# Sixteen gate columns by seven block products instead of eight, with their operands, results and the branch outputs passed through DRAM

## The chip, the core and the metric

The kernel runs on one core of a Trainium2 chip. Five engines work side by side: TensorE (PE in the profile, with its weight loads PEld), VectorE (DVE), ScalarE (ACT), GpSimd (POOL) and SyncE (SP, which here only issues transfers between DRAM and the on-chip memory). The metric is the device time of one execution in microseconds (us); the kernel before has a median of 1602.3 us over three runs.

## The reference

One layer on 1024 tokens of width 1024, all in float32, with 16 meta tokens in front. Only the lines that the change concerns are given:

```python
a = rms_norm(h, norm_mix)
(q_na, k_na, v_na, q_hg, z_f, z_b, i_hg, g_hg, gate_na, gate_hg) = split_cols(a @ w_in)
y_na = neighbourhood_attention(q_na, k_na, v_na, rpb) @ w_na_out      # 512 -> 1024
y_hg = hgrn2_branch(q_hg, z_f, z_b, i_hg, g_hg, ...) @ w_hg_out       # 512 -> 1024
mix = sigmoid(gate_na) * y_na + sigmoid(gate_hg) * y_hg
h = h + mix @ w_o
h = h + square(relu(rms_norm(h) @ w_up)) @ w_down
```

The two gates are a 1024 x 1024 by 1024 x 2048 product: 16 blocks of 128 columns.

## The kernel before

Float32 products are made from three products of a rounded type: each operand is split into `hi` (a rounded copy, a cast on ACT) and `lo` (what is left, a subtraction on DVE), and PE adds hi*hi, hi*lo and lo*hi in one PSUM bank (`mm3`, lines 133 to 135). A weight block is 128 columns of `w_in` (1024 x 128): `load_block` (lines 117 to 125) issues its load on SP's queue into a `raw` tile and makes `hi` and `lo`. Two `raw`, two `hi` and two `lo` tiles of this kind exist (the pool `wp`).

The program has these stages. First the rows are normalised and transposed into `aT` (two tile pairs, for tokens 0 to 511 and 512 to 1023). Then come four HGRN heads (`hgrn`, four times some 85 us). A head doubles its block size over seven levels. At a level PE multiplies 128 x 128 blocks into `sc`, POOL updates `Y` (line 363), DVE makes the next `X` from it (lines 360 and 361) and the queries `QQ` (line 378). Before the levels POOL adds `kd` from `X` and `Y` twice, once for each half of the tokens (line 338), and DVE makes `q` from a projection (line 291). Projections of the next columns stand between these small matmuls as filler. Their results `oT` stay on chip. The neighbourhood attention (NA) follows, two heads at a time in four pairs, and its result `OT` stays on chip too.

The gates are ordinary projections (`gate_proj`, line 632): 16 blocks, each 2 halves of the tokens x 8 slices x 3 = 48 matmuls, 768 in all, and a sigmoid on ACT straight from PSUM into an on-chip tile `sg` (line 636). They are interleaved with the multiplication of the branch outputs by `w_hg` and `w_na`, the stage "mix" (384 matmuls), whose operands `sh` and `sl` are split from `oT` and `OT` on chip. After it come `w_o`, the second norm, `w_up` (which already uses seven block products, lines 797 to 935) and `w_dn`.

A scheduler fixes the order of the instructions on each engine, and on SP's queue, when the program is built. It works from its own estimates of what each costs; every engine then executes its list in that order, and an instruction that waits holds up all those behind it on its engine. (Only the last stage is in an order written by hand.)

Of the kernel before, what the change touches and what calls it, by code (L numbers as in the profile page):

```python
# [46 lines left out]
def layer(ctx: ExitStack, tc: tile.TileContext, x, meta, w_in, w_na, w_hg, w_o, w_up, w_dn,  # L47
# [173 lines left out]
    oTs = ExitStack()  # L221
    oTp = oTs.enter_context(tc.tile_pool(name="oTp", bufs=1, side="right"))
    oT = oTp.tile([P, NHG, T], F32, name="oT")
# [41 lines left out]
    def hgrn(hd, hp, lmask_get, gates, more):  # L265
# [172 lines left out]
        list(more)  # L438
        yield
        for hf in (1, 0):  # L440
# [39 lines left out]
    OTp = oTs.enter_context(tc.tile_pool(name="OTp", bufs=1, side="right", reuse_waits="tile"))  # L480
    psum_pools(mx=1, s=2, t=2, b=1)
    OT = OTp.tile([P, NPAIR, T], F32, name="OT")
    with tc.tile_pool(name="np", bufs=1, reuse_waits="tile") as npl:
# [17 lines left out]
        for p in range(NPAIR):  # L501
# [52 lines left out]
            po = {}  # L554

# [20 lines left out]
            def values(s, i, js, pr):  # L576
# [35 lines left out]
                dst = OT[64 * i:64 * i + 64, p].rearrange("p (r s c) -> p s r c", s=8, c=8)  # L612
# [9 lines left out]
            for st in pend:  # L622
                values(*st)


    psum_pools(mx=3, a=3)
    mixs = ExitStack()
    mixp = mixs.enter_context(tc.tile_pool(name="mixp", bufs=1, reuse_waits="tile"))
    sgp = mixs.enter_context(tc.tile_pool(name="sgp", bufs=4, reuse_waits="tile"))
    mix = mixp.tile([P, KC, T], F32, name="mix")  # L630

    def gate_proj(col):
        sg = sgp.tile([P, T], F32, tag="sg", name="sg")

        def ev(ps, t0, n):
            act.activation(sg[:, t0:t0 + n], ps, AF.Sigmoid)
        proj(col, ev)
        return sg

    gates = []  # L640
# [5 lines left out]
    for br, (wsrc, src) in enumerate(((w_hg, oT), (w_na, OT))):  # L646
        with tc.tile_pool(name="op", bufs=1, reuse_waits="tile") as op_:
            sh = op_.tile([P, 4, T], F32R, name="sh")
            sl = op_.tile([P, 4, T], F32R, name="sl")
            gates_to(8 * br + 2)  # L650
            for k in range(4):
                split(sh[:, k], sl[:, k], src[:, k])
# [68 lines left out]

# [93 lines left out]
    def up_bank(t):  # L815
        return bank(t, t).rearrange("p a b -> p (a b)")
# [389 lines left out]
```

## Time and profile before

| | |
|---|---|
| three runs | 1599.82, 1602.3, 1603.77 us |
| the profiled execution | 1602.57 us, with a span of 1600.4 us from the first to the last instruction (2.2 us lie around it) |
| input and norm | 0 to 38 us |
| HGRN heads, from the first level work on POOL | 38 to 397 us |
| NA | 397 to 615 us, gate matmuls as filler from 580 us |
| the rest of the gates and the mix | 615 to 862 us |
| `w_o`, second norm | 862 to 956 us |
| `w_up` | 956 to 1293 us |
| `w_dn`, last norm | 1293 to 1600 us |

A row of the page's groups or of the timeline names the line, the engine, the operation, output<-inputs with the shapes, and how often; then busy time, the mean time of one, and idle time of the engine before it with what ended it. In the windows view each row is a stretch of the span, with the busy time and the number of instructions of each engine, the granted clock of PE (1.00 is full) and the transfers.

### The profile page before, as it was taken

The page shows a single profiled execution, that of the slowest core. Times are in us where ns is not written, and L with a number is a line of the kernel's source. Part 1 is how long each engine was busy: PE and PEld are TensorE (multiplying, and loading weights), DVE is VectorE, ACT ScalarE, POOL GpSimd, SP SyncE. Part 2 cuts the span into 40 slices and gives each one's busy share as a digit, 9 for nine tenths or more (in the row PEclk, how much of TensorE's full clock was granted, in tenths as well). Part 3 has the DMA queues.
Part 4 walks back from the last instruction along what each step waited for, and adds up shares of the span by engine and source line. Part 5 has one row for each costly group of instructions (what it writes and reads, how often), then busy time and mean ns, then how long its engine had stood idle before and what let it go on. Part 6 is the DMA issues. An engine that isn't in the chain of part 4 may idle for free.

```text
span 1600.4 us, 20348 instructions
## 1 busy us (share of the span) xinstructions
PE 1555.2 (97%) x7876; PEld 1309.3 (82%) x7876; DVE 964.2 (60%) x1524; ACT 607.6 (38%) x1082; POOL 333.9 (21%) x299
## 2 busy tenths in 40 slices
PE   6999999999999999999999998999999999999998
PEld 5788889888888888888887876788888878887886
DVE  6666767565767865123226258766666454779666
ACT  6221121112656654112123035555555443434444
POOL 4322121212011000000000012543333300227033
PEclk9999999999999999999999999999999999999999
DMA  5101001002122111111412123544444477563324
GB/s 184 40 27 40 27 28 40 27 28 68 30 74 63 45 41 40 40 53 53 145 53 78 54 105 113 168 156 163 145 152 145 160 261 234 199 224 118 99 86 145
DMA packets 120625, 158.03 MB, mean 99 GB/s; under 512 B 6337, under 2 KB 80065, under 8 KB 120529
## 3 DMA queue, kind: packets, MB, share of 16 engines
q1 hardware_dynamic: 118624, 150.70, 28.7%
q10 hardware_dynamic: 1584, 4.98, 0.8%
q8 instruction: 62, 1.02, 0.3%
q0 software_dynamic: 320, 1.05, 0.2%
q14 instruction: 35, 0.28, 0.1%
HBM read 118.96 MB, written 37.75 MB: 98 GB/s over the span
## 4 chain that ended last, share of the span: by engine, by line
PE 86%; DVE 7%; issue 3%; ACT 2%; POOL 1%; DMA 1%; DVEq 0%; POOLq 0%; SPq 0%; ACTq 0%
PE mm L134 14%; PE mm L133 13%; PE mm L135 13%; PE mm L949 4%; PE pa L949 4%; PE pc L949 4%; PE sc L351 4%; PE pb L949 3%; PE pb L800 3%; PE pb L802 3%; PE pb L801 3%; PE pc L800 2%; PE pc L801 2%; PE pc L802 2%; PE pa L800 2%
## 5 line engine op out<-in xcount | busy, mean ns | idle before, releaser
L133 PE MATMUL mm<-aT,hi 128*128 128x512 f32 (+2 forms) x896 | 328.6, 367 | 1.2 <-DVE QX L507 1.2
L135 PE MATMUL mm<-aT,lo 128*128 128x512 f32 (+2 forms) x896 | 327.5, 366 | 0.1
L134 PE MATMUL mm<-aT,hi 128*128 128x512 f32 (+2 forms) x896 | 326.6, 364 | 0.0
L133 PEld LDWEIGHTS mm<-aT,hi 128*128 128x128 f32 x896 | 169.6, 189 | 23.5 <-issue 1.4
L135 PEld LDWEIGHTS mm<-aT,lo 128*128 128x128 f32 x896 | 169.4, 189 | 23.1 <-POOL lo L124 0.3
L134 PEld LDWEIGHTS mm<-aT,hi 128*128 128x128 f32 x896 | 169.5, 189 | 22.0
L95 DVE TENSOR_TENSOR dl<-ur,dh 128x1024 fp32r<-128x1024 f32 x55 | 76.5, 1392 | 93.7 <-ACT dh L94 91.8
L94 ACT CAST dh<-ur 128x1024 fp32r<-128x1024 f32 x55 | 57.9, 1053 | 162.3 <-issue 78.1
L123 ACT CAST hi<-raw 128x1024 fp32r<-128x1024 f32 x44 | 46.3, 1053 | 189.0 <-PE mm L134 171.2
L124 DVE TENSOR_TENSOR lo<-raw,hi 128x1024 fp32r<-128x1024 f32 x42 | 51.6, 1230 | 85.8 <-ACT hi L123 85.8
L90 POOL TENSOR_SCALAR rtm<-ssq 128x1 f32<-128x1 f32 (+1 forms) x17 | 7.5, 439 | 397.0 <-ACT junk L754 372.1
L812 DVE TENSOR_TENSOR wl<-sx,wh 128x512 fp32r<-128x512 f32 x70 | 50.0, 722 | 30.7 <-ACT wh L811 30.7
L811 ACT CAST wh<-sx 128x512 fp32r<-128x512 f32 x70 | 42.6, 620 | 64.9 <-PE pc L801 27.3
L812 DVE TENSOR_TENSOR wl<-raw,wh 128x512 fp32r<-128x512 f32 x46 | 50.2, 1091 | 23.8 <-ACT wh L811 23.0
L351 PE MATMUL sc<-QQ,X 128*128 128x128 f32 x448 | 61.7, 288 | 1.5 <-DVE QQ L378 1.2
L351 PEld LDWEIGHTS sc<-QQ,X 128*128 128x128 f32 x448 | 58.2, 196 | 4.4 <-issue 2.0
L363 POOL TENSOR_TENSOR Y<-X,TN 128x512 f32<-128x512 f32 x20 | 33.8, 1691 | 110.3 <-DVE X L360 110.3
L819 ACT ACTIVATE uv<-uv 128x512 f32<-128x512 f32 x48 | 30.4, 633 | 66.4 <-DVE uv L927 49.9
L932 POOL TENSOR_TENSOR us<-u,uv 128x512 f32<-128x512 f32 x15 | 24.3, 1619 | 137.5 <-ACT uv L820 137.5
L569 DVE CUSTOM_DVE_ANT_0 pr<-nsc,NB 128x432 f32<-128x432 f32 (+1 forms) x64 | 35.3, 559 | 28.1 <-PE nsc L564 27.9
L800 PE MATMUL pb<-nt,wh 128*128 128x512 f32 x128 | 50.3, 393 | 2.0 <-DVE uv L920 2.0
L551 POOL TENSOR_TENSOR NB<-NB,bs 128x256 f32<-128x256 f32 (+1 forms) x24 | 19.6, 842 | 156.3 <-DMA NB<-in_wmask 94.1
(331 smaller groups left out, 3906.3 us busy)
## 6 DMA issues: line engine op xcount, KB each, us to landing
ur<-usp SPq DMA_DIRECT2D x55, 512.0 KB, 3.3
raw<-in_w_in SPq DMA_DIRECT2D x48, 512.0 KB, 3.7
raw<-in_w_up SPq DMA_DIRECT2D x16, 1024.0 KB, 6.0
usp<-us SPq DMA_DIRECT2D x60, 256.0 KB, 2.1
w<-in_w_dn SPq DMA_DIRECT2D x16, 512.0 KB, 4.5
usp<-uv SPq DMA_DIRECT2D x30, 256.0 KB, 2.5
xt<-in_x SPq DMA_DIRECT2D x8, 512.0 KB, 9.3
hres<-in_x SPq DMA_DIRECT2D x8, 512.0 KB, 6.5
```

What stands on the lines that cost most here:

```text
L94: act.copy(hi, src)
L95: dve.tensor_tensor(lo, src, hi.bitcast(F32), op=ALU.subtract)
L124: eng.tensor_tensor(lo[:, :kc], raw[:, :kc], hi[:, :kc].bitcast(F32), op=ALU.subtract)
L133: pe.matmul(ps, lh, rh, start=first, stop=False)
L134: pe.matmul(ps, lh, rl, start=False, stop=False)
L135: pe.matmul(ps, ll, rh, start=False, stop=last)
L351: pe.matmul(sc[:, c], X[:, tb + c * P:tb + (c + 1) * P], fap(QQ, tb + c * P, [[2 * h, P // (2 * h)], [T + h, 2], [1, h]]), start=True, sto ...
L800: pe.matmul(ps, lhs[0][:, c], rhs[0][:, k], start=first and k == 0, stop=False, skip_group_check=True)
L801: pe.matmul(ps, lhs[0][:, c], rhs[1][:, k], start=False, stop=False, skip_group_check=True)
L802: pe.matmul(ps, lhs[1][:, c], rhs[0][:, k], start=False, stop=k == 3, skip_group_check=True)
L812: dve.tensor_tensor(v(lo), src, v(hi).bitcast(F32), op=ALU.subtract)
L949: pe.matmul(ps, a[n == 2][:, q, j * P:(j + 1) * P], b[n == 1][:, q], start=first and n == 0, stop=last and n == 2, skip_group_check=True)
```

## The change

Each pair of gate columns (2m, 2m+1) becomes one 2 x 2 block product: two halves of the inner dimension, two halves of the tokens, two column blocks. Strassen's scheme (Winograd's form) needs seven products of 12 matmuls (`chain`) where the plain form needs eight, so 8 x 84 = 672 matmuls in place of 768.

- Sums of the activations (`block_sums`): for each of four slices POOL restores four 128 x 512 blocks from `aT`'s hi and lo (four additions) and makes `t1`, `t2`, `t3`, `t4` of them (four subtractions). One slice is made in each HGRN head, and each result is stored in DRAM (`tsp`).
- Two of the seven products (`first_gates`) need no sums. They are written ahead of the others; the intermediate `g1` stays on chip, and the first sigmoid goes to DRAM.
- The other five (`gate_pair`) need the sums of the activations, read back and split (`second_operand`), and sums of the weights made on DVE (`gate_sums`, four 128 x 512 operations) that are then split. Additions on DVE and one on POOL put the products together before the sigmoid. All gates go to DRAM (`gsp`) and are read back in the mix.
- The branch outputs go to DRAM (`osp`) in place of `oT` and `OT`, and are read back and split ahead of the mix (`branch_operand`). The gates are now finished before the mix begins.

The stages `w_up` and `w_dn` are as before (helpers have only moved up in the file).

The diff, cut to its core:

```diff
-    oTs = ExitStack()
...
-    oT = oTp.tile([P, NHG, T], F32, name="oT")
...
+    def block_sums(k, pool_):
+        r = {}
+        for v, h, kk in (("t1", 0, k), ("t3", 1, k), ("t2", 1, k + 4), ("t4", 0, k + 4)):
+            r[v] = pool_.tile([P, TH], F32, tag="rt", name="rt", bufs=4)
+            hi, lo = (t[:, kk, :TH].bitcast(F32) for t in aT[h])
+            pool.tensor_tensor(r[v], hi, lo, op=ALU.add)
+        pool.tensor_tensor(r["t1"], r["t3"], r["t1"], op=ALU.subtract)
+        pool.tensor_tensor(r["t3"], r["t2"], r["t3"], op=ALU.subtract)
+        pool.tensor_tensor(r["t2"], r["t2"], r["t1"], op=ALU.subtract)
+        pool.tensor_tensor(r["t4"], r["t4"], r["t2"], op=ALU.subtract)
+        for v in r:
+            sp.dma_start(tsp[v][k], r[v])
...
+        block_sums(hd, hp)
...
-            dve.scalar_tensor_tensor(oT[:, hd, hf * TH:(hf + 1) * TH], pt.rearrange("p c t -> p (c t)"),
+            ot = hp.tile([P, TH], F32, tag="ot", name="ot", bufs=2)
+            dve.scalar_tensor_tensor(ot, pt.rearrange("p c t -> p (c t)"),
...
+            sp.dma_start(osp[0][hd][:, hf * TH:(hf + 1) * TH], ot)
...
-    OT = OTp.tile([P, NPAIR, T], F32, name="OT")
...
+            sp.dma_start(osp[1][p], OT)
...
+    g1 = {m: gfp.tile([P, TH], F32, name=f"g1_{m}") for m in reversed(range(NG))}
...
+    def gate_out(c, h, t, src):
+        act.activation(t, src, AF.Sigmoid)
+        sp.dma_start(gsp[c][:, h * TH:(h + 1) * TH], t)
+    def first_gates(ms):
+        blocks, ps = [], []
+        for m in ms:
+            hi, lo = load_block(w_in[:, gate_col(2 * m):gate_col(2 * m) + P], KC)
+            blocks.append([[flat(t)[:, q * TH:(q + 1) * TH] for t in (hi, lo)] for q in range(2)])
+        for m, b in zip(ms, blocks):
+            ps.append(mm_tile())
+            chain(ps[-1], b[0], aV["b11"], True)
+            act.copy(g1[m], ps[-1])
+        for m, b, p in zip(ms, blocks, ps):
+            chain(p, b[1], aV["b21"], False)
+            gate_out(2 * m, 0, gfp.tile([P, TH], F32, tag="go", name="go", bufs=2), p)
...
+    psum_pools(pa=2, pb=2, pc=2)
+    first_gates((0, 1))
+    first_gates((2, 3))
...
+    def second_operand(v):
+        for k in range(4):
+            t = g_tile("gv", TH, bufs=5)
+            sp.dma_start(t, tsp[v][k])
+            split(aV[v][0][:, k], aV[v][1][:, k], t)
...
+    def gate_sums(m):
...
+            c = gate_col(2 * m + q)
+            sp.dma_start(t, w_in[:, c:c + P].rearrange("(k p) c -> p k c", p=P))
+            raw.append(flat(t))
+        sa, sb = g_tile("sx", D, bufs=2), g_tile("sx", D, bufs=2)
+        winograd(dve, raw[0][:, :TH], raw[0][:, TH:], raw[1][:, :TH], raw[1][:, TH:],
+                 sb[:, :TH], sa[:, TH:], sb[:, TH:], sa[:, :TH])
+        W = {}
+        W["s4"], W["s2"] = gate_weights(sa)
+        W["s1"], W["s3"] = gate_weights(sb)
+        W["a22"], = gate_weights(raw[1][:, TH:])
+        return W
+    def gate_pair(m, W, before):
+        pb, pc = up_bank("pb"), up_bank("pc")
+        p3 = g_tile("p3", TH, bufs=2)
+        chain(pc, W["s4"], aV["b22"], True)
+        act.copy(p3, pc)
+        before()
+        chain(pb, W["s2"], aV["t2"], True)
+        u1, u3, u2 = (g_tile("gv", TH, bufs=5) for _ in range(3))
+        dve.tensor_tensor(u1, pb, g1[m], op=ALU.add)
+        chain(pc, W["s1"], aV["t1"], False)
+        dve.tensor_tensor(u1, u1, pc, op=ALU.add)
+        gate_out(2 * m, 1, u1, u1)
+        chain(pb, W["s3"], aV["t3"], False)
+        dve.tensor_tensor(u3, pb, g1[m], op=ALU.add)
+        pool.tensor_tensor(u3, u3, p3, op=ALU.subtract)
+        dve.tensor_tensor(u3, u3, pc, op=ALU.add)
+        gate_out(2 * m + 1, 1, u3, u3)
+        def last():
+            chain(pb, W["a22"], aV["t4"], False)
+            dve.tensor_tensor(u2, pb, g1[m], op=ALU.add)
+            gate_out(2 * m + 1, 0, u2, u2)
+        return last
+    first_gates((4, 5))
+    for v in ("t2", "t1"):
+        second_operand(v)
+    W = gate_sums(0)
+    first_gates((6, 7))
+    for v in ("t3", "t4"):
+        second_operand(v)
+    last = lambda: None
+    for m in range(NG):
+        last = gate_pair(m, W, last)
+        if m + 1 < NG:
+            W = gate_sums(m + 1)
+    last()
+    gps.close()
+    gfs.close()
...
-    def gates_to(n):
-        for m in range(len(gates), min(n, 2 * KC)):
-            gates.append(gate_proj((C_GH if m < KC else C_GN) + (m % KC) * P))
...
-            sl = op_.tile([P, 4, T], F32R, name="sl")
-            gates_to(8 * br + 2)
...
-                split(sh[:, k], sl[:, k], src[:, k])
...
+    def branch_operand(br):
+        for k in range(4):
+            raw = wp.tile([P, KC, P], F32, tag="raw", name="raw")
+            sp.dma_start(flat(raw), osp[br][k])
+            split(*osrc[br, k], flat(raw))
+    branch_operand(0)
+    for br, wsrc in enumerate((w_hg, w_na)):
+        for jj in range(0, KC, 2):
+            raw, hi, lo = (flat(wp.tile([P, KC, P], dt, tag=t, name=t))
+                           for t, dt in (("raw", F32), ("hi", F32R), ("lo", F32R)))
+            sp.dma_start(raw.rearrange("p (k c) -> p k c", k=4),
+                         wsrc[:, jj * P:(jj + 2) * P].rearrange("(k p) c -> p k c", p=P))
+            split(hi, lo, raw)
+            if br == 0 and jj == 2:
+                branch_operand(1)
+            for j in (jj, jj + 1):
+                sg = sgp.tile([P, T], F32, tag="sg", name="sg")
+                sp.dma_start(sg, gsp[8 * br + j])
```

How the rows of an engine stand (its list, in the order of execution), at three places. The first is POOL at the start of HGRN head 0, before the change; `oml_sb` is the last operation of the input stage some rows ahead, `tm` and `km` are small operations on the 16 meta tokens:

```order
L389 TENSOR_TENSOR km_351<-km_351,tm_1039 128x4x2
L389 TENSOR_TENSOR km_351<-km_351,tm_1042 128x2x4
L389 TENSOR_TENSOR km_351<-km_351,tm_1045 128x8
L338 TENSOR_TENSOR kd_607<-X0_348,Y_349 128x512
L338 TENSOR_TENSOR kd_615<-X0_348,Y_349 128x512
L363 TENSOR_TENSOR Y_349<-X0_348,T0_347 128x256x2
L363 TENSOR_TENSOR Y_349<-X_670,TN_522 128x128x4
```

The same place with the change, from the fourth slice's sums on (`rt` are the tiles of `block_sums`; lines 356 and 381 are 338 and 363 of before):

```order
L232 TENSOR_TENSOR rt_3249<-aT00_90,aT01_91 128x512
L232 TENSOR_TENSOR rt_3251<-aT10_92,aT11_93 128x512
L234 TENSOR_TENSOR rt_3249<-rt_3251,rt_3249 128x512
L232 TENSOR_TENSOR rt_3253<-aT10_92,aT11_93 128x512
L356 TENSOR_TENSOR kd_653<-X0_386,Y_387 128x512
L232 TENSOR_TENSOR rt_3255<-aT00_90,aT01_91 128x512
L235 TENSOR_TENSOR rt_3251<-rt_3253,rt_3251 128x512
L381 TENSOR_TENSOR Y_387<-X0_386,T0_385 128x256x2
L236 TENSOR_TENSOR rt_3253<-rt_3253,rt_3249 128x512
L237 TENSOR_TENSOR rt_3255<-rt_3255,rt_3253 128x512
L381 TENSOR_TENSOR Y_387<-X_708,TN_560 128x128x4
```

All 32 operations of the four calls of `block_sums` have moved to this place: behind `oml_sb` 28 of them stand ahead of the second `kd` (8 of these ahead of the first), 2 more ahead of the first `Y`, and the last 2 ahead of the second `Y`. Through the levels of all four heads the lists of PE and of DVE hold the same rows as before, but for the name of the output tile.

The second place is the start of the five products, where SP's list before the change held only loads of weight blocks:

```order
L121 DMA raw_5886<-in_w_in 128x8x128
L121 DMA raw_5953<-in_w_in 128x8x128
L121 DMA raw_6012<-in_w_in 128x8x128
L658 DMA raw_6070<-in_w_hg 128x4x256
L121 DMA raw_6133<-in_w_in 128x8x128
```

Now ACT's list there, with `go` the gate results of `first_gates` blocks 4 and 5, `gv` the sums read back, `sx` the weight sums of pair 0 (made of raw_6201 and raw_6203):

```order
L685 ACTIVATE go_6151<-mm_6111 128x512
L94 CAST at10_6093<-gv_6189 128x512
L94 CAST at10_6093<-gv_6193 128x512
L685 ACTIVATE go_6166<-mm_6125 128x512
L94 CAST at10_6093<-gv_6197 128x512
L94 CAST hi_6215<-sx_6206 128x1024
L94 CAST hi_6211<-sx_6205 128x1024
```

The sigmoid of block 5 now stands ahead of the last sum's cast and of the weight casts of pair 0. On DVE the four weight sums stand behind the split of that last sum, and on SP raw_6203 is issued behind the store of go_6151. PE's list has 68 matmuls of `first_gates` between NA's last one and the first product of pair 0.

The third place is the start of the mix, on ACT; before the change the splits of the branch operand stood between sigmoids of gates:

```order
L636 ACTIVATE sg_6551<-mm_6584 128x512
L123 CAST hi_6747<-raw_6746 128x1024
L94 CAST sh_6676<-OT_3202 128x1024 x4
L636 ACTIVATE sg_6686<-mm_6693 128x512
```

Now, from the last gate (gv_7062) to the first `w_hg` block (raw_7164):

```order
L685 ACTIVATE gv_7061<-gv_7061 128x512
L685 ACTIVATE gv_7062<-gv_7062 128x512
L94 CAST o000_7145<-raw_7148 128x1024
L94 CAST o010_7143<-raw_7152 128x1024
L94 CAST o020_7141<-raw_7156 128x1024
L94 CAST o030_7139<-raw_7160 128x1024
L94 CAST hi_7165<-raw_7164 128x1024
```

The four operand casts and the first weight cast of the mix stand behind the sigmoid of the very last gate; no matmul stands on PE between that gate's product and the first of the mix, which uses hi_7165. All five `raw` tiles come from the two of the pool `wp`, so raw_7156 is loaded into raw_7148's place, and raw_7164 into raw_7156's.

More of the change, by code (lines that the diff above doesn't have):

```diff
@@ L554, in layer @@
             po = {}
+            OT = npl.tile([P, T], F32, tag="OT", name="OT", bufs=2)
             def scores(s, i):
@@ L677, in layer @@
+    ops_.close()
     hresp = ExitStack()
@@ L794, in a_tile @@
         return pool_.tile([P, n], dt, tag=tag, name=tag, bufs=bufs)
-    def chain(ps, lhs, rhs, first):
-        for k in range(4):
-            c = slice(k * P, (k + 1) * P)
-            pe.matmul(ps, lhs[0][:, c], rhs[0][:, k], start=first and k == 0, stop=False, skip_group_check=True)
-            pe.matmul(ps, lhs[0][:, c], rhs[1][:, k], start=False, stop=False, skip_group_check=True)
-            pe.matmul(ps, lhs[1][:, c], rhs[0][:, k], start=False, stop=k == 3, skip_group_check=True)
     w_pools = [upa]
```

106 lines of the change are left out of this document (62 added, 44 removed).

## The prediction

> **What bounds the kernel now.** I read the page's busy times and chain of waits first, then the windows by stage.
>
> ```profile
> PE 1555.2 (97%) x7876; PEld 1309.3 (82%) x7876; DVE 964.2 (60%) x1524; ACT 607.6 (38%) x1082; POOL 333.9 (21%) x299
> PE 86%; DVE 7%; issue 3%; ACT 2%; POOL 1%; DMA 1%; DVEq 0%; POOLq 0%; SPq 0%; ACTq 0%
> 700.00:800.00 100.00, 100.00 (x443) 82.81 (x442) 27.77 (x30) 20.51 (x27) 0.00 (x0) 1.00 0.27 90
> 1020.00:1060.00 40.00, 40.00 (x177) 33.12 (x177) 26.30 (x35) 21.03 (x37) 19.85 (x13) 1.00 0.50 170
> ```
>
> PE is busy 97% of the span and is 86% of the chain that ends last. In the gates and the mix (700 to 800 us) it never pauses: 100 us for 443 matmuls of 128x512, 0.2257 us each. In w_up, where seven products are already in use with sums on DVE and POOL beside them, it is full too (1020 to 1060 us). So a matmul less is worth its 0.2257 us, if nothing makes PE wait. Since PE has no slack, what decides is whether the added work makes it wait, and the places to look at are those where PE hangs on another engine. The tightest is the start of head 0:
>
> ```profile
> 38.02 0.20 POOL L175 TENSOR_TENSOR oml_sb<-lt,mx 128x8 f32<-128x8 f32 x1
> ...
> 42.26 1.31 POOL L338 TENSOR_TENSOR kd<-X,Y 128x512 f32<-128x512 f32 x1
> ...
> 51.69 1.23 DVE L124 TENSOR_TENSOR lo<-raw,hi 128x1024 fp32r<-128x1024 f32 x1 [3.23 <-ACT hi L123]
> ...
> 53.81 1.22 DVE L277 TENSOR_TENSOR TN<-T 128x1024 f32<-128x1024 f32 x1
> 53.97 4.55 POOL L338 TENSOR_TENSOR kd<-X,Y 128x512 f32<-128x512 f32 x1 [10.40 <-DVE X L245]
> ...
> 54.95 0.42 DVE L360 COPY X<-Y 128x512 f32<-128x512 f32 x1
> 55.28 0.69 DVE L277 TENSOR_TENSOR TN<-TN 128x512 f32<-128x512 f32 x1
> 55.89 1.14 DVE L361 TENSOR_TENSOR X<-X,T 128x512 f32<-128x512 f32 x1
> 56.92 0.43 DVE L277 TENSOR_TENSOR TN<-TN 128x256 f32<-128x256 f32 x1
> ...
> 58.61 1.85 POOL L363 TENSOR_TENSOR Y<-X,T 128x512 f32<-128x512 f32 x1
> ...
> 60.49 0.43 DVE L360 COPY X<-Y 128x512 f32<-128x512 f32 x1 [3.14 <-POOL Y L363]
> ...
> 61.04 0.68 DVE L291 TENSOR_TENSOR q<-q,mm 128x512 f32<-128x512 f32 x1
> ...
> 61.87 1.13 PE L341 MATMUL sc<-q,kd 128*128 128x128 f32 x8 [0.20 <-DVE q L291]
> ```
>
> Here POOL idles 10.4 us, then makes the second kd and the first Y. DVE waits 3.14 us for that Y, its next rows make q, and PE waits for q. That this wait of PE is only 0.20 us means that everything on the path POOL Y, DVE X, DVE q, PE sc is already just in time: whatever delays Y delays PE by as much.
>
> **The change part by part.** *The matmuls.* 768 become 672: 96 x 0.2257 = 21.7 us off PE. This is the whole gain.
>
> *The sums of the activations*, 32 on POOL. Two rows give the price of one (minimum, median, maximum of kd; mean of the w_up difference):
>
> ```profile
> L338 POOL TENSOR_TENSOR kd<-X,Y x8: 1314/1322/4554, 42.3 to 309.4; 128x512 f32<-128x512 f32 x8
> L933 POOL TENSOR_TENSOR us<-uv 128x512 f32<-128x512 f32 x15 | 19.4, 1292 | 37.3 <-ACT uv L820 37.3
> ```
>
> I take 1.31 us (1.28 as the lower bound). By POOL's new list 30 of them stand ahead of the first Y. From 38.2 us, where oml_sb ends, POOL has 30 x 1.31 = 39.3, the small km operations 2.4 (all that it did before the first kd, up to 42.26), two kd 2.6, and Y 1.85: 46.2 us, so Y would end at 84.4. On top comes DVE. The second kd took 4.55 us in place of 1.31, 3.24 more, and DVE was busy from 53.81 to 57.35: POOL got nothing done beside DVE operations with two inputs on chip. Those in this stretch (two lo, of which the second is shown, three TN, one X copy, one X product) add 2 x 1.23 + 1.22 + 0.69 + 0.43 + 0.42 + 1.14 = 6.4 us: Y ends at 90.7. If every DVE operation of 38 to 57 us blocked POOL it would be some 10.7 us and 95; if none did and a sum took 1.28, 83.5. I take 90.7, as the 4.55 row speaks for blocking and I have no row for the others. DVE's X copy waits for Y with q behind it in its list, PE's sc waits for q, so PE stands still for 90.7 - 60.5 = 30.2 us. Two further sums stand ahead of the next Y (2.6 us, of which I count 1.3, for DVE has other rows to run meanwhile): 31.5 us, bounds 23 and 38. SP's list carries the stores of these sums ahead of three weight loads, but those loads are needed after the stall. Nothing gives it back: behind it PE is the bound again. The first sum cannot start earlier, for it needs all of aT, and the last of aT's lo is written just before oml_sb.
>
> [...]
>
> *From NA to the five products.* Count from the end of NA's last matmul. 68 first_gates matmuls (68 x 0.2257 = 15.3 us) cover the loading and splitting of the sums and of pair 0's weights. But ACT's sigmoid of gate block 5 waits for the last of the 68 and stands ahead of the last sum's cast and of both weight casts. Durations:
>
> ```profile
> L636 ACT ACTIVATE sg<-mm 128x512 f32<-128x512 f32 x32 | 18.9, 594 | 59.5 <-PE mm L135 57.4 <-PE pov L609 1.1 <-issue 1.0
> L811 ACT CAST wh<-sx 128x512 fp32r<-128x512 f32 x70 | 42.6, 620 | 64.9 <-PE pc L801 27.3 <-PE pa L801 19.4 <-PE pb L801 12.5
> L812 DVE TENSOR_TENSOR wl<-sx,wh 128x512 fp32r<-128x512 f32 x70 | 50.0, 722 | 30.7 <-ACT wh L811 30.7
> L94 ACT CAST hi<-raw 128x1024 fp32r<-128x1024 f32 x8 | 8.4, 1054 | 35.1 <-PE mm L134 35.1
> L95 DVE TENSOR_TENSOR lo<-raw,hi 128x1024 fp32r<-128x1024 f32 x8 | 9.8, 1225 | 64.3 <-ACT hi L94 64.3
> ```
>
> 15.5 + 0.59 (sigmoid) + 0.62 (cast) + 0.72 (its split) + 4 x 0.72 (weight sums) = 20.3; cast of s4/s2 to 21.4; DVE first splits s1/s3 (20.3 to 21.5), then s4/s2 to 22.8. PE does two matmuls at 21.4 and the rest from 22.8: 7 us idle. raw_6203 is issued after block 4's store and lands about as late, for which I add 0.5.
>
> Then the clock. An earlier wait of that length shows what follows:
>
> ```profile
> 989.65 0.50 PE L800 MATMUL pb<-nT,wh 128*128 128x512 f32 x1 [3.96 <-ACT wh L811]
> ...
> 991.60:993.00 1.40, 1.40 (x4) 1.14 (x4) 1.40 (x3) 0.08 (x1) 0.00 (x0) 0.50 0.05 12
> 993.00:994.00 1.00, 1.00 (x4) 0.78 (x3) 1.00 (x3) 0.00 (x0) 0.00 (x0) 0.55 0.11 25
> ```
>
> After 3.96 us of idling PE ran at half clock for some 3.4 us, which is 1.7 us lost. So this place costs 7.5 + 1.7 = 9.2 us (bounds 4, if the sums land early and the clock holds, and 12, if one more load is in the way).
>
> *The loop of eight pairs.* Per pair PE has 60 matmuls, 13.5 us; DVE four sums 2.9, splits 2 x 1.225 + 0.72, five additions of some 0.7: 9.6 us; ACT two casts 2.1, one 0.62, one copy and three sigmoids 2.4: 5.1 us; POOL 1.3. The weight sums of a pair stand a pair ahead. The w_up window above (DVE 26.3, POOL 19.9 of 40) ran without an idle microsecond with more on POOL, so I count nothing. If that cover failed, it would be some 2 us in each of seven pairs.
>
> *From the last gate to the mix.* Before, sh and sl were split under gate matmuls, so it cost nothing. Now nothing stands on PE in between, and the casts stand behind the last gate's sigmoid. The loads:
>
> ```profile
> ur<-usp SPq DMA_DIRECT2D x55, 512.0 KB, 3.3
> raw<-in_w_hg SPq DMA_DIRECT2D x4, 512.0 KB, 3.5
> out<-hr SPq DMA_DIRECT2D x16, 256.0 KB, 2.0
> ```
>
> From the end of the last product: addition on DVE 0.8 (with 0.1 to start), sigmoid to 1.4, cast of slice 0 to 2.45, its split to 3.7, which frees a raw tile; slice 2 is read back in 3.3, to 7.0; cast 8.05, split 9.3, frees the tile for w_hg's block: 3.5, to 12.8; cast 13.85 (PE does two matmuls), split 15.1. PE idles 14.6 us, and 1.7 for the clock: 16.3 us. Bounds: 11 with loads at the 2.0 us of the fastest row and no loss of clock, 19 with some 0.4 us more for each transfer queued on SP. The rest of the mix keeps its 384 matmuls; its reloads come a block ahead.
>
> *Small ones.* The start of w_o:
>
> ```profile
> 863.62 0.73 PE L133 MATMUL mm<-wh,mT 128*128 128x512 f32 x2 [1.14 <-ACT wh L94]
> ```
>
> The casts of w_o's first half wait no longer for the mix's last matmul, since their tiles lie where branch 0's operand was: -1 us (-1.7 to +3, for two of the w_o loads now stand behind an x load that waits for the mix). Two table loads more on ACT in NA's last pair, under filler: 0 (to 2.6). The stores of ot and OT: 0, nothing waits on them within 100 us.
>
> **Sum:** -21.7 + 31.5 + 9.2 + 16.3 - 1 = +34.3 us. Against the profiled execution (1602.57, 0.3 us above the median of the runs) that is 1637 us. With all lower bounds: -21.7 + 23 + 4 + 11 - 1.7 = +15, 1617; with all upper: -21.7 + 38 + 12 + 19 + 3 + 2.6 = +53, 1655.
>
> **Rivals.** *The sums on POOL hide (not slower).* POOL idled 10.4 us there. For Y not to be late, 30 sums must fit in 60.5 - 38.2 - 2.4 - 2.6 - 1.85 - 6.4 = 9 us: it turns at 0.30 us a sum. Small operations on POOL do take that (oml_sb 0.20), but no row of 128x512 is under 1.28. Time: -21.7 + 9.2 + 16.3 - 1 = +2.8, 1605.
>
> *Only head 0 stalls.* The two hand-overs could be covered if the read-backs came earlier than I follow them through the lists; for it speaks that the scheduler put them far ahead on SP; against it ACT's order. -21.7 + 31.5 - 1 = +8.8, 1611.
>
> *Everything hides*, the change is worth its matmuls: 1581. It needs both.
>
> *The loop is bound by DVE and its locks on POOL*: seven pairs at 2 us more, 1651. For it: the 4.55 us row; against it: the full w_up window.
>
> **How the numbers follow.** Forecast 0.70 (own range 1617 to 1655); loop bound 0.10; head 0 alone 0.10; sums hidden 0.04; all hidden 0.06. Faster by over 0.3% (4.8 us, about what a measurement of this kernel can tell from none) has the last case and a little of the one before it, 0.07; within it 0.05; slower 0.88. The range runs from 1608, so that "head 0 alone" is in, to 1655: the two hidden cases and a little at the top lie outside.
>
> **What would show it.** In the changed kernel's timeline of POOL, 30 operations of some 1.3 us each between 38 us and the first Y, and that Y ending near 91; PE's first sc near 92 with some 30 us of idling before it, released by DVE's q. Then PE idle for some 7 us before the first matmul on pc, released by ACT, and some 14 us before the first matmul on o0, with w_hg's load before it on the chain; a granted clock of 0.5 behind each. 96 matmuls fewer, and a full PE from pair 1 to pair 7. It is wrong if sums take under 1 us, if Y ends before 75, or if either hand-over shows under 3 us.

## The result: 47 us slower, and the profile after

The changed kernel takes 1649.26 us (median of four runs, 1648.5 to 1653.85) against 1602.05 us before: 47.2 us more, a ratio of 1.0301 with a 95% interval from 1.0279 to 1.0324. The forecast was 1637 us, with a range up to 1655. The sign and the places are those of the forecast; the size is 12 us above it, and this section and the next ones ask where these come from.

The changed kernel's page has the 96 matmuls less, and a PE that is busy for 10.7 us less in a span that is 46.3 us longer (1646.7 us). PE's share of the chain that ends last falls from 86% to 78%:

```profile
PE 1544.5 (94%) x7780; PEld 1296.0 (79%) x7780; DVE 1058.4 (64%) x1628; ACT 641.9 (39%) x1132; POOL 385.9 (23%) x339
PE 78%; DVE 9%; POOL 4%; issue 3%; DMA 3%; ACT 3%; SPq 0%; DVEq 0%; POOLq 0%; ACTq 0%
```

PE busy for 10.7 us less and not for 21.7 already says that some of its matmuls ran slower. The waits of PE, longest in total first (us in total, how often, the longest), name the three stalls:

```profile
PE sc L359 <- DVE q L309: 31.0, 2, 29.1
PE mm L133 <- ACT hi L94: 16.0, 1, 16.0
PE pt L109 <- DVE na L105: 11.7, 4, 10.1
PE pc L664 <- ACT hi L94: 9.3, 2, 8.3
```

The third row stands in the kernel before too (11.6 us). The first was 2.5 us there; the second and the fourth are new. The stretches below are read off the first and last rows of PE's timeline that bear the name (us; all of them from the one profiled execution of each kernel):

| stretch | before | after | difference |
|---|---|---|---|
| start to the first `sc` of head 0 | 61.9 | 87.6 | +25.7 |
| to the last transposition of the heads | 323.3 | 324.4 | +1.1 |
| to the end of NA | 230.4 | 238.4 | +8.0 |
| to the first matmul of `w_o` | 248.0 | 257.0 | +9.0 |
| to the last matmul | 729.5 | 731.7 | +2.2 |

The third stretch holds 13 matmuls of 128x512 more than before (417 against 404), the fourth 109 fewer. At 0.2257 us each that is +2.9 and -24.6. So what was lost beside the matmuls is 26.8 us in the heads, 5.1 in NA, 33.6 in the gates and the mix, and 2.2 behind them: 67.7 us against a gain of 21.7.

**Head 0.** The sums (tile `rt`) in two windows up to the end of the first Y, before and after DVE ran dry (each row: start and end, length, then POOL's busy time on `rt` with the count, the granted clock, and the transfers; the two operations at the edge are counted in both rows, and one that begins at 84.01 is in the second), and the rows around that Y in the timeline:

```profile
35.00:63.40 28.40, 23.99 (x17) 1.00 0.18 66
63.40:84.10 20.70, 17.58 (x16) 0.50 0.42 139
```

```profile
35.05 5.09 POOL L232 TENSOR_TENSOR rt<-aT,aT 128x512 f32<-128x512 f32 x4
...
53.44 1.45 DVE L263 TENSOR_SCALAR X<-sn,oml_sb 128x256 f32<-128x256 f32 x1
...
71.13 1.26 POOL L236 TENSOR_TENSOR rt<-rt 128x512 f32<-128x512 f32 x1
...
82.34 1.74 POOL L381 TENSOR_TENSOR Y<-X,T 128x512 f32<-128x512 f32 x1
84.11 1.47 DVE L378 COPY X<-Y 128x512 f32<-128x512 f32 x1 [20.39 <-POOL Y L381]
...
87.59 2.05 PE L359 MATMUL sc<-q,kd 128*128 128x128 f32 x8 [29.13 <-DVE q L309]
```

This is the path of the forecast: 30 sums on POOL (24.0 + 17.6, less 0.1 of the one at 84.01: 41.5 us), Y, DVE's copy (which waited 3.14 us before and 20.39 now), q, and PE, which waits 29.13 us in place of 0.20. The last row also says that the eight small matmuls take 2.05 us in place of 1.13: PE comes back at half clock (a granted clock of 0.50 from 87.59 to 90.90 us).

**From NA to the five products, and from the last gate to the mix.** Rows of several engines in order of time:

```profile
664.82 0.50 SPq L737 DMA_DIRECT2D raw<-in_w_in  x1
665.93 0.60 ACT L685 ACTIVATE go<-mm 128x512 f32<-128x512 f32 x1 [0.61 <-PE mm L666]
668.87 0.62 ACT L94 CAST at<-gv 128x512 fp32r<-128x512 f32 x1 [2.35 <-DMA gv<-tsp_t]
670.38 0.69 DVE L655 TENSOR_TENSOR sx<-raw 128x512 f32<-128x512 f32 x1 [0.17 <-DMA raw<-in_w_in]
671.71 1.04 ACT L94 CAST hi<-sx 128x1024 fp32r<-128x1024 f32 x1 [2.22 <-DVE sx L657]
674.13 0.80 PE L664 MATMUL pc<-aT,hi 128*128 128x512 f32 x1 [8.29 <-ACT hi L94]
...
801.77 0.63 ACT L685 ACTIVATE gv<-gv 128x512 f32<-128x512 f32 x1 [1.06 <-DVE gv L768]
802.31 1.97 ACT L94 CAST o<-raw 128x1024 fp32r<-128x1024 f32 x2
809.97 1.04 ACT L94 CAST o<-raw 128x1024 fp32r<-128x1024 f32 x1 [5.69 <-DMA raw<-osp]
811.26 1.04 ACT L94 CAST o<-raw 128x1024 fp32r<-128x1024 f32 x1 [0.25 <-DMA raw<-osp]
815.83 1.04 ACT L94 CAST hi<-raw 128x1024 fp32r<-128x1024 f32 x1 [3.52 <-DMA raw<-in_w_hg]
816.93 0.80 PE L133 MATMUL mm<-o,hi 128*128 128x512 f32 x1 [15.97 <-ACT hi L94]
```

At the first place the sigmoid (665.93) is not what decides. The second weight load is issued at 664.82, behind a store and behind eight of the sixteen reads of the sums, and DVE's first weight sum starts only when it has landed, at 670.38, 4.5 us behind the last filler matmul. At the second place the chain is the one of the forecast, link by link: sigmoid, two casts, read-back, two casts, `w_hg`, cast, PE after 15.97 us.

The clock behind it (windows; the column behind POOL is the granted clock):

```profile
801.00:817.00 16.00, 0.07 (x1) 0.07 (x1) 5.59 (x6) 5.64 (x6) 0.00 (x0) 0.60 0.84 282
817.00:825.00 8.00, 7.96 (x25) 5.96 (x26) 4.18 (x4) 3.12 (x3) 0.00 (x0) 0.73 0.47 158
```

25 matmuls in the eight microseconds behind the wait, where a full clock makes 35. (A part of this is a wait for the first block's lo; the section on the clock takes the two apart.)

### The profile page after: what moved, and what is told of

Read it like the earlier page. It is cut to its first block, busy times and chain, and to the rows that moved or that the text cites. A ratio compares the mean times of both kernels' runs of the same rounds, so it can differ in the third digit from the quotient of the medians.

```text
span 1646.7 us, 20670 instructions
## 1 busy us (share of the span) xinstructions
PE 1544.5 (94%) x7780; PEld 1296.0 (79%) x7780; DVE 1058.4 (64%) x1628; ACT 641.9 (39%) x1132; POOL 385.9 (23%) x339
## 4 chain that ended last, share of the span: by engine, by line
PE 78%; DVE 9%; POOL 4%; issue 3%; DMA 3%; ACT 3%; SPq 0%; DVEq 0%; POOLq 0%; ACTq 0%
PE mm L134 9%; PE mm L135 9%; PE mm L133 9%; PE mm L1084 4%; PE pa L1084 4%; PE pb L664 4%; PE pb L666 4%; PE pb L665 4%; PE pc L1084 3%; PE sc L369 3%; PE pb L1084 3%; PE pc L666 3%; PE pc L664 2%; PE pc L665 2%; PE pa L664 2%
## 5 line engine op out<-in xcount | busy, mean ns | idle before, releaser
L133 PE MATMUL mm<-aT,hi 128*128 128x512 f32 (+2 forms) x640 | 229.3, 358 | 2.3 <-DVE QX L528 2.3
L135 PE MATMUL mm<-aT,lo 128*128 128x512 f32 (+2 forms) x640 | 228.0, 356 | 0.0
L134 PE MATMUL mm<-aT,hi 128*128 128x512 f32 (+2 forms) x640 | 227.3, 355 | 0.0
L133 PEld LDWEIGHTS mm<-aT,hi 128*128 128x128 f32 x640 | 122.4, 191 | 15.0 <-issue 2.4
L135 PEld LDWEIGHTS mm<-aT,lo 128*128 128x128 f32 x640 | 122.1, 191 | 13.1
L134 PEld LDWEIGHTS mm<-aT,hi 128*128 128x128 f32 x640 | 122.1, 191 | 12.6
L123 ACT CAST hi<-raw 128x1024 fp32r<-128x1024 f32 x36 | 37.8, 1050 | 127.1 <-PE mm L134 87.2
L133 PE MATMUL mm<-o,hi 128*128 128x512 f32 x128 | 50.7, 396 | 16.0 <-ACT hi L94 16.0
L124 DVE TENSOR_TENSOR lo<-raw,hi 128x1024 fp32r<-128x1024 f32 x34 | 44.8, 1317 | 26.4 <-ACT hi L123 26.2
L762 POOL TENSOR_TENSOR gv<-gv,p 128x512 f32<-128x512 f32 x8 | 12.2, 1519 | 195.1 <-DMA raw<-in_w_in 105.7
L572 POOL TENSOR_TENSOR NB<-NB,bs 128x256 f32<-128x256 f32 (+1 forms) x24 | 19.6, 843 | 159.5 <-DMA NB<-in_wmask 149.3
L1174 POOL TENSOR_TENSOR w<-w,tt 128x512 f32<-128x512 f32 x16 | 23.3, 1455 | 134.0 <-DVE tt L1173 119.4
```

The lines of the kernel that those rows point to most:

```text
L124: eng.tensor_tensor(lo[:, :kc], raw[:, :kc], hi[:, :kc].bitcast(F32), op=ALU.subtract)
L133: pe.matmul(ps, lh, rh, start=first, stop=False)
L134: pe.matmul(ps, lh, rl, start=False, stop=False)
L135: pe.matmul(ps, ll, rh, start=False, stop=last)
```

## The experiments

All times below stand beside the changed kernel's 1649.26 us and the kernel before's 1598.7 to 1603.4 us, its median in each group of runs. Runs with one number were timed once.

### Is it POOL's operations that PE waits for in head 0?

The first three runs ask this. The first leaves the operations out and keeps their stores:

```diff
     def block_sums(k, pool_):
-        (eight operations on POOL into rt, four stores of rt)
+        for v, h, kk in (("t1", 0, k), ("t3", 1, k), ("t2", 1, k + 4), ("t4", 0, k + 4)):
+            sp.dma_start(tsp[v][k], aT[h][0][:, kk, :TH].bitcast(F32))
```

> Against the changed kernel (1649 us). The 32 operations of block_sums on POOL are left out; 16 rounded halves of the activations are stored in DRAM in their place, so that the same number of stores stands on SP and the gates are computed from wrong operands (that part of the result is left out). Theory A (POOL's operations ahead of the first Y are what PE waits for): POOL's list is that of the kernel before, the first sc starts near 62 us as there (87.6 with the sums), the wait of 29 us for q goes, and the time falls by 26 to 29 us, to some 1622. Rival B (the 16 stores of the sums delay the weight loads on SP, or the transfers slow the rest): PE still waits 20 us or more ahead of the first sc and the time stays above 1640.

1620.69 us: 28.6 less. The first `sc` starts at 61.16 us, after a wait of 0.24 us, as before the change:

```profile
61.16 1.13 PE L347 MATMUL sc<-q,kd 128*128 128x128 f32 x8 [0.24 <-DVE q L297]
```

The heads end at 384.5 us (385.2 before the change, 412.0 with it, 27.6 later), although all 16 stores are still there. Theory A stands, rival B falls.

The second run keeps 16 of the 32 operations:

```diff
-        pool.tensor_tensor(r["t1"], r["t3"], r["t1"], op=ALU.subtract)
-        (and the three other subtractions)
```

> The 16 additions of block_sums stay, the 16 subtractions are left out (the gates get wrong operands). All 16 stand ahead of the second kd. Theory A with a fixed price of each (1.40 us, what 30 of them measured): the first Y ends at 35.1 + 16 x 1.40 + 2.8 (km) + 2.6 (two kd) + 1.75 = 64.7 us in place of 84.1, the first sc starts near 68, PE waits some 6 to 9 us there, and the time is some 20 us below the changed kernel: 1629. Rival C (the first sums pay for DVE's operations beside them, the later ones run alone at 1.26 us): the first Y later than that, at 66 or more, and the gain 18 us or less.

1627.58 us, 21.7 less; `sc` waits 9.52 us and starts at 70.28 us, 17.3 us earlier than with all sums. The group of the sums ahead of the first Y (count, busy time, mean ns), and the row of that Y:

```profile
L232 POOL TENSOR_TENSOR rt<-aT,aT 128x512 f32<-128x512 f32 x16 | 24.1, 1539 | 0.0
...
67.10 1.77 POOL L377 TENSOR_TENSOR Y<-X,T 128x512 f32<-128x512 f32 x1
```

Y ends 31.5 us behind the start of the first sum, not the 29.6 of a fixed price. Sixteen sums take 1.54 us each here. In the changed kernel the sums that run when DVE has run dry take 1.26 us (the row at 71.13). So rival C is right on the price: a sum costs some 0.25 us more while DVE works beside it. On the total it erred by 4 us (18 or less, where 21.7 were measured), in part since the profiles of the two also differ by 1.5 us at the start of NA, where half clock follows a wait in the one and not in the other (last section).

The third run is a mended kernel: the sums stay, but behind the last level of their head.

```diff
-                pool.tensor_tensor(fap(KB, h, hv), ...)
+                last_y[0] = pool.tensor_tensor(fap(KB, h, hv), ...)
...
-        block_sums(hd, hp)
+        with tc.issue_after(last_y[0].ins):
+            block_sums(hd, hp)
```

> Nothing is left out: the eight operations of each head's block_sums are issued on POOL behind the last level operation of that head, where POOL idled 32 us before the change, so that none stands ahead of the first Y. Theory A: first sc near 62 us, time 1649 - 27 = 1622 (1619 to 1626). Rival D (the sums cost wherever they stand, since they block DVE's two-input operations and so the next step of the head): each head gets 2 to 10 us longer, 1630 to 1650.

1619.94 us (ratio to the kernel before 1.0105, 1.009 to 1.012): 29.3 less. That is the 26.8 us that the sums had cost, and some 1.6 us ahead of NA, where half clock follows a wait in the changed kernel's profile and not in this one (last section). The timeline of POOL in head 0 shows them in the gap behind the levels:

```profile
100.96 6.00 POOL L232 TENSOR_TENSOR rt<-aT,aT 128x512 f32<-128x512 f32 x4
...
111.75 1.63 POOL L237 TENSOR_TENSOR rt<-rt 128x512 f32<-128x512 f32 x1
132.95 0.20 POOL L90 TENSOR_SCALAR st<-ss 128x4 f32<-128x4 f32 x1 [19.57 <-DVE ss L465]
```

POOL is done 19.6 us before its next operation can start. The stretch from the first `sc` to the end of the heads is 324.8 us in place of 323.3 before the change: 32 operations cost 1.5 us in this place and 27 in the other. Rival D falls.

### Is the start of the mix the chain of reads and splits?

Branch 0's operand is read and split during gate pairs 2 to 5, into the first half of `aT`, which nobody reads any more by then:

```diff
+    osrc = {(0, k): [fap(aT[0][q], 2 * k * UW[0], [[1, T]]) for q in range(2)] for k in range(4)}
+    def first_operand(k):
+        for h in range(2):
+            t = g_tile("gv", TH, bufs=5)
+            c = slice(h * TH, (h + 1) * TH)
+            sp.dma_start(t, osp[0][k][:, c])
+            split(osrc[0, k][0][:, c], osrc[0, k][1][:, c], t)
     for m in range(NG):
+        if 2 <= m < 6:
+            first_operand(m - 2)
...
-    branch_operand(0)
```

> Nothing is left out: branch 0's operand is read back and split during gate pairs 2 to 5 into the place of the first half of aT, which is free by then, and the first weight blocks of the mix can be split ahead of the last gate. The rest is as in the changed kernel. Theory A (the 16 us before the first matmul on o are the chain of loads and splits behind the last gate): the wait falls below 2 us, no half clock follows it, and the time is 1649 - 16 - 2.5 = 1630 to 1632. Rival E (the wait only moves: the next thing late is the mix's own weights or its result tile, whose memory the last gate holds): a wait of 5 us or more stays between the last gate and the second block of the mix, 1636 to 1645.

1623.99 us (1.0128, 1.0112 to 1.0145): 25.3 less, 6 to 8 more than expected. The window from just after the last gate's product (798.6 us) to just ahead of `w_o`:

```profile
800.00:884.00 84.00, 84.00 (x372) 69.59 (x371) 54.17 (x73) 22.89 (x29) 0.00 (x0) 1.00 0.59 198
```

PE is full. From the end of NA to `w_o` it is 236.7 us in place of 257.0: 20.3 less, mainly the wait of 16.0, the slow start behind it (2.3), and the wait of 0.88 us ahead of `w_o` that is gone. `w_o` and the second norm take 95.6 us in place of 98.5; PE waits for no block of `w_o` there any more, where the changed kernel has three such waits (1.95 us). I had not expected that part. Of the rest, 1.5 us lie ahead of NA, where this profile too has no half clock. Rival E falls.

### What is late ahead of the first gate pair?

The forecast had put it on ACT's order, the trace names the load. Two runs take these apart. The first only moves the two weight loads of pair 0 ahead of the reads on SP:

```diff
+    raw0 = gate_raw(0)
     for v in ("t2", "t1"):
         second_operand(v)
-    W = gate_sums(0)
+    W = gate_sums(0, raw0)
```

> Nothing is left out. The two weight loads of gate pair 0 are issued on SP ahead of the eight reads of the sums, in place of behind them; the rest is written as in the changed kernel. In ACT's list one weight cast now stands ahead of the sigmoids of blocks 4 and 5, but the cast of s4 and s2, which the first product needs, still stands behind the sigmoid of block 5 and one cast of a sum. Theory A2 (what the traces show last is the load of the second weight block, which landed 4.5 us after the last filler matmul): the wait of 8.3 us ahead of the first product on pc falls to 2.5 to 4 us, what sigmoid, cast and cast take behind the last filler, and with less of half clock behind it the time falls by 4 to 8 us, to 1641 to 1645. Rival F (my prediction's chain: ACT's sigmoid of block 5 ahead of the casts sets the end, and the load is only about as late): the wait stays at 6 us or more, 1647 or more.

1643.6 us, and the wait is 3.00 us in place of 8.29:

```profile
665.32 0.59 ACT L685 ACTIVATE go<-mm 128x512 f32<-128x512 f32 x1
665.80 0.61 ACT L94 CAST at<-gv 128x512 fp32r<-128x512 f32 x1
666.31 1.05 ACT L94 CAST hi<-sx 128x1024 fp32r<-128x1024 f32 x1
...
667.41 0.65 PE L664 MATMUL pc<-aT,hi 128*128 128x512 f32 x1 [3.00 <-ACT hi L94]
```

Now it is sigmoid, cast, cast, the chain that I had forecast, and it is worth 3 us. The other 5.3 us were the load: theory A2, rival F falls. (One weight cast has moved ahead of the sigmoids as well, but the one that the first product needs has not.) The second run puts the whole of the weight sums first, so that the cast too stands ahead of the sigmoid:

```diff
+    W = gate_sums(0)
     for v in ("t2", "t1"):
         second_operand(v)
-    W = gate_sums(0)
```

> Nothing is left out. The weight sums of gate pair 0 and their splits are written ahead of the reads of the sums of the activations, so that their loads come first on SP and the cast of s4 and s2 stands ahead of the sigmoid of block 5 on ACT. Theory A2: the first product starts right behind the last filler (wait below 1 us), no half clock follows, and the time falls by the wait of 8.3 us, by some 2 us of half clock and by some of the short waits in pair 0: 1636 to 1640. If the reads of the sums are now late in its place (rival G: the first product waits less, the next ones for t2 and t1 as much more), the stage from the end of NA to the end of the gates gets shorter by less than 4 us, 1645 or more.

1638.24 us (1.0227, 1.0214 to 1.024): 11.0 less. The wait is 1.06 us, just above the 1 us that was expected:

```profile
665.67 0.50 PE L664 MATMUL pc<-aT,hi 128*128 128x512 f32 x1 [1.06 <-ACT hi L94]
```

No half clock follows, and from the end of NA to the end of the gates it is 140.8 us in place of 150.6. Rival G falls. The 596 matmuls of that stretch are worth 134.5 us, so 16.1 us were lost there and 6.3 still are: in short waits ahead of the first two pairs and in them, and 1.0 ahead of the last product of the last pair, which waits for DVE (0.78 us) in both kernels.

### Do the three add up?

All three mends in one kernel:

> Nothing is left out: sums behind the levels, weight sums of pair 0 first, and branch 0's operand read ahead, all three together. If the three stalls and the half clock behind each are the whole loss and add up, the time is 1649.3 - 29.3 (sums) - 25.3 (operand) - 10 to 13 (gate start) = 1582 to 1585, under the kernel before by 18 to 20 us (96 matmuls less are worth 21.7). Rival H (the stages are coupled: a transfer or a POOL operation that had room in the stalls is late when they are gone): 1590 or more.

1586.71 us (six runs, 1584.01 to 1589.97), 62.6 less than the changed kernel, and below the kernel before: ratio 0.9907, 0.9893 to 0.9922, so 0.9% faster. The three alone had given 29.3 + 25.3 + 11.0 = 65.6. (The profiles of all three lack the 1.5 us of half clock ahead of NA that the changed kernel's has, so the sum may count these 1.5 us three times; that would be the whole difference, but no run tests it.) The expected 1582 to 1585 was 2 us too low; it is not rival H's 1590. Its page has PE as busy as the kernel before, with the 96 matmuls less:

```profile
PE 1535.6 (97%) x7780; PEld 1290.5 (81%) x7780; DVE 1050.9 (66%) x1632; ACT 641.6 (41%) x1136; POOL 395.9 (25%) x339
```

Of the 21.7 us it keeps 15.9. From the end of the heads to the end of NA it takes 236.3 us, 3.0 more than the 230.4 of before with 13 matmuls more; from there to `w_o` 227.4, 4.0 more than 248.0 less 109 matmuls. I have not followed these 7 us further.

### What does the clock cost by itself?

The 60 matmuls of this run fill most of the wait ahead of the mix, with work that nobody needs:

```diff
     last()
+    with tc.issue_after(end[0].ins):
+        for n in range(5):
+            chain(up_bank("pa"), [t[:, n, :TH] for t in aT[0]], aV["b11"], True)
```

> The changed kernel with 60 matmuls more: five chains on the first half of aT into a PSUM bank that nobody reads, behind the last gate's product and ahead of the first matmul on o. They take 60 x 0.2257 = 13.5 us of the 16.0 us in which PE waited there. Nothing else moves. If half clock behind a wait is a price of its own, and PE's own work keeps it away: the first matmul on o comes as late as before (16 us behind the last product), the granted clock stays at 1.00, the stage from there to w_o falls from 90.5 us to 87 to 88, and the time by 2 to 4 us, to 1645 to 1647, with more work in it. If the slow stretch comes from something else (operands still being split, transfers), the stage stays at 90 us or more and the time at 1649.

1647.76 us (1.0294, 1.0274 to 1.0314), 1.5 us less than the changed kernel, with runs that overlap, and a miss: the stage from the first matmul on o to `w_o` takes 90.6 us, as without them. The gap that was left open, a second wait right behind it, and a window:

```profile
812.53 0.50 PE L133 MATMUL mm<-o,hi 128*128 128x512 f32 x1 [2.54 <-ACT hi L94]
...
813.79 0.50 PE L135 MATMUL mm<-o,lo 128*128 128x512 f32 x1 [0.53 <-DVE lo L95]
...
815.00:818.00 3.00, 3.00 (x9) 2.32 (x8) 1.25 (x2) 0.91 (x1) 0.00 (x0) 0.50 0.77 254
```

Behind the gap of 2.54 us and the wait of 0.53 us for the block's lo the clock falls as far as behind the gap of 16 us (to 0.50 in both), and only some two microseconds after work has begun again. So the last run fills the gap (six chains in place of five):

> As the run before, with 72 added matmuls in place of 60: 72 x 0.2257 = 16.25 us, so that they reach over the whole wait of 16.0 us in place of leaving 2.5 us of it open. If an idle gap of some 2.3 us is enough to bring half clock on and its price does not depend on the gap's length (what the run before suggests: half clock from 815 to 818.5 us after a gap of 2.54 us, as after 16 us), then without a gap the granted clock stays at 1.00 from the last gate to the mix, the first matmul on o comes 16.2 to 16.5 us behind the last product, and the stage from it to w_o takes 87 to 88 us in place of 90.5. If the slow start of the mix has another cause, the stage stays at 90 us or more.

```profile
820.23 0.50 PE L133 MATMUL mm<-o,hi 128*128 128x512 f32 x1 [0.29 <-ACT hi L94]
...
803.60:820.20 16.60, 16.33 (x73) 13.18 (x71) 5.51 (x5) 5.68 (x6) 0.00 (x0) 1.00 0.81 285
820.20:828.00 7.80, 7.78 (x34) 6.46 (x35) 4.97 (x5) 3.02 (x3) 0.00 (x0) 1.00 0.42 139
```

The clock stays at 1.00 and the stage takes 88.2 us in place of 90.5, just above what was expected (87 to 88). These 2.3 us are not the clock alone. In this run's order the first product with the block's lo (L135) is the seventh matmul of the mix and not the third, so that PE no longer waits for the split of the first block, where the run before waited 0.53 us for it. By the starts of the matmuls, the run before loses 1.6 us to half clock (8 matmuls in 3.4 us, 0.43 us each in place of 0.2257) and 0.7 us to the wait for lo and the restart behind it. So the price of the clock by itself is 1.6 us at this place. The time, 1649.46 us in one run, shows nothing of it: the operand was ready later (the first matmul on o comes 17.0 us behind the last product, not the 16.2 to 16.5 expected, and still waits 0.29 us for ACT), and the start of the program took 2.7 us longer in this profile.

## Why the prediction was right, and where it was off

The sign, the range and the three places came as forecast, and at the first and the third also what waits there for what; at the second the forecast chain is only 3 of 8.3 us. The rivals fell: the sums did not hide (1605), the two hand-overs were not covered (1611), the change was not worth its matmuls alone (1581), and the loop is not DVE's: between 770 and 790 us, PE is full (90 matmuls in 20 us). The sum, term by term, in us, against the profiled execution:

| term | forecast | measured | from |
|---|---|---|---|
| matmuls | -21.7 | -21.7 | 7876 less 7780, at 0.2257 |
| sums on POOL in head 0 | +31.5 | +26.8 | stretches; 27.6 by the end of the heads without POOL's operations |
| heads to the end of NA | 0 | +5.1 | stretch less 13 matmuls |
| NA to the five products, clock and loop | +9.2 | +16.1 | 150.6 less 596 matmuls |
| last gate to the mix, clock | +16.3 | +18.3 | wait 16.0; behind it 2.3, clock and a wait for lo |
| start of `w_o` and behind | -1 | +2.2 | stretch |
| sum | +34.3 | +46.8 | spans: +46.3 |

The terms come out 0.5 us above the spans, since the kernel before had lost a little at these places too.

**The sums** were mis-sized by 4.7 us, and in both directions. Each took 1.38 us (41.5 for 30) in place of my 1.31 plus the 6.4 us for DVE's operations, which would be 1.52; Y ended 49.0 us behind the start of the first sum and not 52.5; and that start came at 35.1 us and not 38.2, because the input stage was 3 us faster in this profile (its last transposition ended anywhere between 32.6 and 36.2 us in the eleven profiles). Against these stands what I had left out: DVE is slowed as well. Its copy behind Y took 1.47 us in place of 0.43, and half clock on the return took about 1 us. I had counted DVE operations with two on-chip inputs, and one copy, as the only ones that block; yet X from sn and oml_sb (one large input) took up to 1.45 us beside the sums and 0.35 alone. That operations of these kinds alone block POOL was my estimate, and no run shows it or the 6.4 us; what the runs show in its place is a sum of 1.50 to 1.54 us beside a busy DVE, and of 1.26 us when DVE has run dry.

**From NA to the products**, the wait was 8.3 us where I said 7.5, but for another reason: my step "sigmoid, cast, weight sums" is 3 us of it (the run with the loads first), and the 0.5 us that I gave to the late raw_6203 is 5.3. What failed is the sentence that the 15.3 us of `first_gates` matmuls cover the loading: the second weight block landed 4.5 us behind the last of them. The reads of the sums are what delays it: seven of them were issued ahead of the first load and an eighth ahead of the second, and the DMA engines are full (1.07, the number before the last in the window). A read took 4.4 us (median); the only row of that size that I had shown, a store, took 2.0:

```profile
665.00:670.00 5.00, 0.84 (x4) 0.38 (x2) 1.52 (x3) 1.53 (x3) 0.00 (x0) 1.00 1.07 344
```

```profile
gv<-tsp_t SPq DMA_DIRECT2D x16, 256.0 KB, 4.4
```

That the size of the wait agreed is luck. The step that failed in its size is the loop, "so I count nothing": it holds from pair 2 on up to the last product, but the stretch took 7.6 us more than its matmuls (127 us for 528) where I had 1.7 for the clock. Over 6 of them are the half clock and the short waits of the first two pairs, and 1.0 is the wait for DVE ahead of the last product.

**The mix** was right in mechanism and within 2 us. The 1.7 us for the clock agree with the 1.6 of the run with 60 matmuls; the wait for the loads and splits was 16.0 us in place of 14.6.

**What I held to be free** was not. Ahead of the gates 5.1 us were lost: the wait for QX grew from 1.19 to 2.25 us (the runs do not show why), half clock followed it (1.5 us), and gate matmuls waited for their weights (0.33 and 0.53 us); the remaining 1.7 us I have not traced. Behind the mix it is 2.2 us where I had -1: the first wait for a block of `w_o` fell only from 1.14 to 0.88 us, and the later ones are 1.4 us longer. I had the late blocks of `w_o` as an upper bound alone. These two and the loop make 14 us; the other terms, the sums above all, take 2 back, which leaves the 12.

## What to carry to other kernels

A scheduler that fills an idle engine with work that is ready will put it in front of work that is not ready yet but urgent; before an operation is called hidden, look at what stands behind it in its engine's list and how much slack that has (here 0.20 us on PE, while the same 32 operations cost 1.5 us further on). Work taken off a full engine is worth its time only if every hand-over is still covered: leave some of the full engine's independent work for each of them, or read operands ahead into memory that is already free. And of a chain with two arms that end at about the same time, give each arm its own upper bound, since mending the one only uncovers the other.

## What the runs showed of the hardware

- The price of a gap on PE is not only its length. Gaps of 2.54 us, 8.3 us and 16 us were each followed by 3.4 to 4.4 us of work at half clock (a granted clock of 0.50), a loss of 1.6 us where it was isolated. Behind a wait of some 2.25 us both were measured. PE waits so long for QX ahead of NA in the changed kernel (2.25 us), and half clock followed; it waits as long in the run with the sums behind the levels (2.25), in that with the operand ahead (2.25) and in that with the weight loads first (2.26), and there half clock did not follow and the stretch up to NA is 1.5 us shorter. In the changed kernel, and in the first of the mended ones (the row of PE, then windows):

```profile
418.30 0.36 PE L133 MATMUL mm<-aT,hi 128*128 128x272 f32 x1 [2.25 <-DVE QX L528]
415.16:418.58 3.42, 1.17 (x10) 0.99 (x9) 2.99 (x6) 2.44 (x6) 0.00 (x0) 1.00 0.61 183
418.58:421.99 3.41, 3.41 (x17) 3.41 (x16) 0.61 (x2) 0.00 (x0) 0.00 (x0) 0.50 0.87 322
```

```profile
391.90 0.36 PE L133 MATMUL mm<-aT,hi 128*128 128x272 f32 x1 [2.25 <-DVE QX L529]
387.07:390.48 3.41, 2.58 (x22) 2.38 (x20) 2.53 (x4) 2.33 (x6) 0.00 (x0) 1.00 0.28 96
390.48:393.89 3.41, 1.99 (x16) 2.02 (x17) 2.13 (x4) 1.68 (x4) 0.00 (x0) 1.00 1.06 348
393.89:397.30 3.41, 3.41 (x22) 3.02 (x21) 0.58 (x2) 1.38 (x5) 2.09 (x3) 1.00 0.37 147
```

  In the granted clocks of the traces before and after the change, every stretch of half clock up to the last matmul lasts 3.41 us or a whole multiple of it (6.83, 17.07 and 27.31 us), and within a trace all of them begin on one grid of that step; the windows above have that length. In the changed kernel the whole gap of 2.25 us lies in one step of the grid (PE busy 1.17 of 3.42 us), and the next step runs at half clock. In the mended one the edge of the windows at 390.48 cuts the gap in two, none of them has more than 1.43 us of idling, and the clock stays at 1.00. Counted over the traces before and after (from their first clock records at 24.5 and 19.2 us on, steps at full clock), each of the eight steps in which PE idled for 2.0 us or more was followed by half clock; of the others one was, with 1.85 us, while one with 1.91 us was not. That the place of a gap on the grid decides what follows is my reading of these rows; no run moves a gap along it.
- DVE and POOL slowed each other: a 128x512 addition took 1.26 us on POOL alone and 1.50 to 1.54 us beside a busy DVE, while short operations of DVE took up to 1.1 us longer beside the sums (1.45 us in place of 0.35, 1.47 in place of 0.43).
